# Output projection of a hybrid encoder as a software pipeline over token tiles in fixed order

## The chip, the cores and the metric

The kernel runs on one core of one Trainium2 chip. The metric is the device time of one execution in microseconds (us); the smaller, the better. The program before was run three times: 2376.43, 2377.62 and 2380.9 us, median 2377.62.

## What is computed

Two request groups (prompt and sample, 1024 tokens of 1024 channels each, float32) go through two layers with shared weights: one attention layer (l=0) and one pooling layer (l=1). Cut from the reference:

```python
for l in range(DEPTH):                      # DEPTH = 2
    mod = jax.nn.silu(c) @ ada_w[l] + ada_b[l]
    shift, scl, gate = jnp.split(mod[:, None, :], 3, axis=-1)
    h = _rmsnorm(x, pre_norm[l]) * (1.0 + scl) + shift
    if l % 2 == 0:
        m = _attn_mixer(h, ...)             # ends in y @ w_out
    else:
        m = _pool_mixer(h, ...)             # u, gate = split(h @ w_in); pooled means; gate; y @ w_out
    x = x + gate * _rmsnorm(m, post_norm[l])
```

_rmsnorm divides each token by the root of its mean square and multiplies by a row. Here x after layer 0 is called x1, and the output projection is `y @ w_out` of layer 0 with all that follows it up to h of layer 1.

## The kernel before

Products are made in float32r pairs: each operand is split into a high part and the rest (hi, lo), and one product is three matmuls. `run()` works through four blocks: attention of the prompt group (s=0) and its output projection, attention of the sample group (s=1) and its output projection, then layer 1 of the sample group and layer 1 of the prompt group. `outproj0(s, ...)` (L995) is the output projection. While it works for s=0, it also prepares the attention input of the sample group from x_sample (tiles xo); for s=1 it does not.

It loops over NT = 8 tiles of 128 tokens. For each tile:

- PE forms y @ w_out in PSUM: `out_mm` (L941), for 8 blocks k of channels 6 matmuls of 512 columns, 48 in all (L945 to L947). Tiles 0 and 1 were made ahead, at the end of attention (`out_pre`, L949), whose split y also serves tiles 2 and 3; for tiles 4 to 7 y is loaded and split in `load_y` (L937 to L939).
- ACT squares the result with a sum along each token (L1061), POOL makes the reciprocal root (`rstd`, L123 and L125), DVE multiplies by the gate row (L1063) and adds into the tile xt, which held x (L1064). SP stores xt to DRAM as x1 (L1065).
- `h_tile` (L250 to L265) then norms x1 for layer 1 **in place in xt**: square on ACT (L250), scaling by row g1 on DVE (L252), adding row sh1 on POOL, or on DVE for the last two tiles (L253), eight transposes on PE in two groups (L258), copies to SBUF on ACT (L263) and, where the result is a matmul operand, its lo part on DVE (L265). Since L252 writes what the store L1065 reads, it waits for that store. In s=0 a second `h_tile` does the same for xo with rows g0 and sh0.

For s=1 the results go straight into hT, layer 1's input. For s=0 the halves go to DRAM as a stash (hs_d, 16 stores, L281), and `layer1(0)` reads them back by token tile (L1081), copies hi on ACT (L1083) and forms lo on DVE, some on POOL (L1084). Layer 1 then multiplies hT with its first weights (`lin_both`, L1091 to L1093), copies the first products on ACT (L1122), and works on in four channel groups; the sums of the last output projection of the group before (L1210, L1229 and L1230) fall into the same time.

The engines' order is set by a scheduler, which the language runs over the whole program from the order of the code and its own model of durations. `run_h` (L1019) is a generator that issues the transposes of finished tiles between the matmuls of a later tile. `prefetch` loads and converts weights of the next stage between matmuls (ws, L290 and L291). Each engine runs its instructions in the order that the scheduler left, and SP issues all DMAs, also in that order. A pool with `bufs=n` has n buffers under a tag; a tile that needs a buffer waits until what was in it is used up. xt has two, xo two, yh two, y0 two.

Of the kernel before, what the change touches and what calls it, by code (L numbers as in the profile page):

```python
# [59 lines left out]
class Trunk:  # L60
    def __init__(self, ctx, tc, t):
# [9 lines left out]
        self.pin = False  # L71
# [18 lines left out]
        self.hs_d = self.dram.tile([NT, 2, P, 4, P], F32, name="hs_d")  # L90
# [153 lines left out]

    def h_tile(self, pool, x, g, sh, idm, put, junk=None, eng=None):
        nc = self.nc
        ss = pool.tile([P, 1], F32, name=self.n("ss"), tag="ss", bufs=6)
        if junk is None:
            junk = pool.tile([P, D], F32, name=self.n("jk"), tag="jk", bufs=2)
        nc.scalar.activation(junk, x, AF.Square, accum_out=ss)  # L250
        r = self.rstd(pool, ss, D, 1)
        nc.vector.scalar_tensor_tensor(x, x, r, g, op0=ALU.mult, op1=ALU.mult)  # L252
        (eng or nc.gpsimd).tensor_tensor(x, x, sh, ALU.add)  # L253
        for b in range(2):
            T = self.ptile("T")
            for k in range(4):
                kk = 4 * b + k
                x_ = nc.tensor.transpose(T[:, k * P : (k + 1) * P], x[:, kk * P : (kk + 1) * P], idm)  # L258
                if k == 0 and self.pin:
                    self.tc.keep_in_program_order(x_)  # L260
            hi, lo, done = put(b)
            Tv = T.rearrange("p (k c) -> p k c", k=4)
            nc.scalar.activation(hi, Tv, AF.Copy)  # L263
            if lo is not None:
                nc.vector.tensor_tensor(lo, Tv, hi.bitcast(F32), ALU.subtract)  # L265
            if done:
                done()
            yield

    @staticmethod  # L270
    def put_hT(hT, i):
        def put(b):
            c = slice(i * P, (i + 1) * P)
            return hT[:, 4 * b : 4 * b + 4, 0, c], hT[:, 4 * b : 4 * b + 4, 1, c], None

        return put

    def put_stash(self, pool, i):
        def put(b):
            hl = pool.tile([P, 4, P], F32, name=self.n("hl"), tag="hl", bufs=2)  # L280
            return hl, None, lambda: self.nc.sync.dma_start(self.hs_d[i, b], hl)  # L281

        return put
# [289 lines left out]
    def layer0(self, s, hT, ap, side, after_proj, open2, run_h, first=None):  # L573
# [28 lines left out]
        if s == 1:  # L602
            self.psum("B", "J")
            self.psum("C", "J")
            self.psum("A", "JJ")
            self.raw = [ap.tile([P, 4, 256], F32, name=self.n("raw"), tag="P", bufs=3) for _ in range(2)]
            for f in range(2):
                nc.sync.dma_start(self.raw[f], self.t["win"][9][:, 4 * f : 4 * f + 4, :])
            next(gens[0])
            self.pin = True  # L610
            for _ in gens[0]:
                run_h(1)
            run_h(40)
            self.pin = False
            open2()
# [378 lines left out]

    def outproj0(self, s, wo, op, hN, pre, prefetch):  # L995
# [4 lines left out]
        hq = []  # L1000
        ys, xt, xo = {}, {}, {}

        def load(i):
            if i < NT:
                xt[i] = op.tile([P, D], F32, name=self.n("xt"), tag="xt", bufs=2)
                nc.sync.dma_start(xt[i], xsrc[i])
                if i >= 4:
                    ys[i] = []
                    for f in range(2):
                        y0 = op.tile([P, 4, P], F32, name=self.n("y0"), tag="y0", bufs=2)  # L1010
                        ys[i].append(op.tile([P, 2, 4, P], F32R, name=self.n("yh"), tag="yh", bufs=2))
                        self.load_y(s, i, y0, ys[i][f], 4 * f, 4 * f + 4, 0)

        def load_o(i):
            if s == 0 and i < NT:
                xo[i] = op.tile([P, D], F32, name=self.n("xo"), tag="xo", bufs=2)
                nc.sync.dma_start(xo[i], xos[i // 2, i % 2])

        def run_h(c):  # L1019
            for _ in range(c):  # L1020
                while hq:
                    try:
                        next(hq[0])
                        break
                    except StopIteration:
                        hq.pop(0)

        perm = op.tile([P, P], F32, name=self.n("perm"), tag="perm")
        g1, sh1 = (self.row(op, x) if s == 1 else None for x in ("g1", "sh1"))
        pg = self.mrow(op, 0, s, 2, "pg")  # L1030
        load(0)
        load(1)
        load_o(0)
        if s == 0:
            g0, sh0 = self.mrow(op, 0, 1, 1, "g0"), self.mrow(op, 0, 1, 0, "sh0")
        load(2)
        g1, sh1 = self.mrow(op, 1, s, 1, "g1", g1), self.mrow(op, 1, s, 0, "sh1", sh1)
        nc.sync.dma_start(perm, t["k_perm"])
        pf = prefetch(op)
        for i in range(NT):  # L1040
            if i >= 2:
                load(i + 1)
            load_o(i + 1)
            if i < 2:
                ps = pre[0][i]
                run_h(4)
            else:
                ps = self.ptile("S")
                for k in range(KT):
                    yh, q = (pre[1][i], k) if i < 4 else (ys[i][k // 4], k % 4)  # L1050
                    self.out_mm(ps, yh, q, wo, k, k == 0, k == KT - 1)
                    if k % 2 == 1:
                        run_h(1)
                        if i >= 4:
                            next(pf, None)
            if s == 0:
                jx = op.tile([P, D], F32, name=self.n("jx"), tag="jx", bufs=1)
                hq.append(self.h_tile(op, xo[i], g0, sh0, self.ident, self.put_hT(hN, i), jx))
            ss = op.tile([P, 1], F32, name=self.n("ss"), tag="ss", bufs=6)
            jk = op.tile([P, D], F32, name=self.n("jk"), tag="jk", bufs=1)  # L1060
            nc.scalar.activation(jk, ps, AF.Square, accum_out=ss)  # L1061
            r = self.rstd(op, ss, D, 1)
            nc.vector.tensor_tensor(jk, ps, pg, ALU.mult)  # L1063
            nc.vector.scalar_tensor_tensor(xt[i], jk, r, xt[i], op0=ALU.mult, op1=ALU.add)  # L1064
            nc.sync.dma_start(x1o[i], xt[i])  # L1065
            put = self.put_stash(op, i) if s == 0 else self.put_hT(hN, i)
            hq.append(self.h_tile(op, xt[i], g1, sh1, perm, put, jk, nc.vector if i >= NT - 2 else None))
        for _ in pf:
            pass
        return run_h  # L1070

    def layer1(self, s, hT, lp, hp, run_h, open_l2):
# [4 lines left out]
        if s == 0:  # L1077
            for i in range(NT):
                h = lp.tile([P, 2, 4, P], F32, name=self.n("h"), tag=("sg1", "wa")[i % 2], bufs=2)
                for b in range(2):  # L1080
                    nc.sync.dma_start(h[:, b], self.hs_d[i, b])  # L1081
                    hi, lo = (hT[:, 4 * b : 4 * b + 4, e, i * P : i * P + P] for e in range(2))
# [465 lines left out]
```

## Time and profile before

| | |
|---|---|
| median of three runs | 2377.62 us |
| profiled execution, span on the core | 2374.5 us |
| the part of the median outside that span | 3.1 us |
| PE busy | 2152.6 us, 91% |
| DVE busy | 1569.9 us, 66% |
| ACT busy | 1062.9 us, 45% |
| POOL busy | 1026.7 us, 43% |
| DMA, mean over the span | 77 GB/s |

The profile is of one execution, of which the span is recorded; the 3.1 us are the difference of the median to it. PE is the matmul engine, PEld its weight loads, DVE, ACT and POOL the vector, scalar and general engines, SP the one that issues DMAs (SPq in a row). "[6.87 <-DMA xt<-xp]" behind a row says that the engine stood idle for 6.87 us before it and that the load of xt from xp ended this. PEclk is the clock that was granted to PE, as a share of 2.4 GHz; 0.50 is its other level, 1.2 GHz. The two output-projection stages lie at 800 to 978 us (s=0) and 1650 to 1798 us (s=1); layer 1 of the prompt group begins at about 2060 us.

### The profile page before, as it was taken

To read this page: it belongs to the slowest core of one execution; us is meant where nothing else is said; L and a number is where in the kernel's file an instruction comes from. 1 tells how busy PE (TensorE), PEld (TensorE's weight loads), DVE (VectorE), ACT (ScalarE), POOL (GpSimd) and SP (SyncE) were. 2 spreads that over 40 slices of the span, in tenths; PEclk is the share of its full clock that TensorE was granted. 3 is DMA by queue.
4 is the path that set the end of the run, shared out by engine and by line. 5 is a ranking of instruction groups with operands and counts; after the bars stand their busy time and mean duration, and the time that the engine had idled before them with its cause. 6 is when DMAs were issued, how large, how long until landed. Compare 5 with 4: busy or idle time off the path is not lost.

```text
span 2374.5 us, 38597 instructions
## 1 busy us (share of the span) xinstructions
PE 2152.6 (91%) x13777; PEld 1907.4 (80%) x13777; DVE 1569.9 (66%) x3453; ACT 1062.9 (45%) x2451; POOL 1026.7 (43%) x1455
## 2 busy tenths in 40 slices
PE   5999899999997866899999999988678999999998
PEld 3988788899997655898898999987457888778887
DVE  7788887767778344677878767775344454693536
ACT  6355555766665333355657666664221111310112
POOL 3675663135344253553321234433223345483552
PEclk9999999999997887999999999989789999999999
DMA  6123222112113444210011112124222111441113
GB/s 253 41 65 95 79 86 69 35 54 71 54 47 106 128 134 131 79 37 17 19 34 37 42 57 69 50 82 116 90 73 85 44 45 53 151 164 40 55 44 146
DMA packets 146561, 182.84 MB, mean 77 GB/s; under 512 B 13944, under 2 KB 109280, under 8 KB 146368
## 3 DMA queue, kind: packets, MB, share of 16 engines
q1 hardware_dynamic: 146032, 179.91, 24.1%
q8 instruction: 109, 1.79, 0.3%
q14 instruction: 84, 0.69, 0.1%
q10 hardware_dynamic: 144, 0.26, 0.0%
q0 software_dynamic: 192, 0.20, 0.0%
HBM read 142.33 MB, written 37.99 MB: 76 GB/s over the span
## 4 chain that ended last, share of the span: by engine, by line
PE 53%; DMA 15%; DVE 15%; issue 7%; POOL 6%; ACT 4%; SPq 0%; POOLq 0%; DVEq 0%; ACTq 0%
PE J L355 5%; PE J L357 5%; PE J L356 5%; PE S L1091 4%; PE S L1093 4%; PE S L1092 4%; DMA x_d<-xt 3%; PE H L676 3%; DMA xt<-xp 3%; POOL w L291 3%; PE T L714 2%; DVE E L694 2%; PE S L1186 2%; PE S L1188 2%; PE S L1187 2%
## 5 line engine op out<-in xcount | busy, mean ns | idle before, releaser
L291 POOL TENSOR_TENSOR w<-ws,w 128x256 fp32r<-128x256 f32 (+1 forms) x418 | 391.0, 949 | 360.0 <-DVE w L290 267.1
L355 PE MATMUL J<-w,hT 128*128 128x256 f32 x1664 | 482.5, 290 | 3.2 <-ACT xj L368 2.3
L357 PE MATMUL J<-w,hT 128*128 128x256 f32 x1664 | 477.5, 287 | 4.1 <-DVE hT L1312 3.9
L356 PE MATMUL J<-w,hT 128*128 128x256 f32 x1664 | 477.7, 287 | 0.4 <-POOL w L291 0.4
L355 PEld LDWEIGHTS J<-w,hT 128*128 128x128 f32 x1664 | 318.7, 192 | 7.2 <-ACT xj L368 3.7
L357 PEld LDWEIGHTS J<-w,hT 128*128 128x128 f32 x1664 | 318.5, 192 | 6.8 <-DVE hT L1312 4.6
L356 PEld LDWEIGHTS J<-w,hT 128*128 128x128 f32 x1664 | 318.5, 191 | 2.9 <-POOL w L291 0.9
L693 ACT ACTIVATE E<-T 128x512 fp32r<-128x512 f32 x384 | 226.8, 598 | 207.4 <-PE T L714 67.3
L694 DVE TENSOR_TENSOR E<-T,E 128x512 fp32r<-128x512 f32 x384 | 261.6, 682 | 84.5 <-ACT E L693 82.3
L290 DVE CAST w<-ws 128x256 fp32r<-128x256 f32 (+1 forms) x420 | 196.6, 493 | 169.5 <-PE S L1093 86.0
L683 ACT ACTIVATE P<-H,mx 128x512 f32<-128x512 f32 x256 | 173.7, 685 | 109.9 <-DVE mx L678 95.2
L1093 PE MATMUL S<-hT,w 128*128 128x512 f32 x512 | 200.5, 392 | 2.0 <-POOL w L291 2.0
L1091 PE MATMUL S<-hT,w 128*128 128x512 f32 x512 | 200.7, 392 | 0.0
L1092 PE MATMUL S<-hT,w 128*128 128x512 f32 x512 | 200.3, 391 | 0.0
L677 DVE TENSOR_REDUCE mx<-H 128x1 f32<-128x512 f32 x256 | 173.7, 681 | 34.1 <-PE H L676 32.0
L714 PE MATMUL T<-identr,P 128*128 128x128 f32 x1024 | 162.6, 274 | 6.9 <-DVE mr L151 3.2
L727 PE MATMUL O<-E,v 128*128 128x256 f32 x512 | 142.8, 301 | 14.1 <-DVE E L694 13.5
L793 ACT ACTIVATE P<-H,nm 128x256 f32<-128x256 f32 x256 | 117.7, 474 | 81.2 <-DVE nm L787 81.0
L726 PE MATMUL O<-E,v 128*128 128x256 f32 x512 | 146.1, 294 | 3.9 <-DVE X L748 2.2
L714 PEld LDWEIGHTS T<-identr,P 128*128 128x128 f32 x1024 | 122.4, 141 | 23.9 <-DVE mr L151 3.4
L441 POOL TENSOR_TENSOR hl<-xj,hl 128x256 fp32r<-128x256 f32 x64 | 48.2, 756 | 206.6 <-DVE hl L440 149.5
L727 PEld LDWEIGHTS O<-E,v 128*128 128x128 f32 x512 | 96.8, 189 | 27.2 <-DVE E L694 24.5
(264 smaller groups left out, 5228.8 us busy)
## 6 DMA issues: line engine op xcount, KB each, us to landing
ws<-win SPq DMA_DIRECT2D x192, 128.0 KB
ws<-ada_w SPq DMA_DIRECT2D x128, 128.0 KB
ws<-pwin SPq DMA_DIRECT2D x60, 256.0 KB
vb<-v_d SPq DMA_DIRECT2D x64, 144.0 KB
xt<-xp SPq DMA_DIRECT2D x16, 512.0 KB
ada<-ada_w SPq DMA_DIRECT2D x16, 512.0 KB
y_d<-X SPq DMA_DIRECT2D x32, 256.0 KB
v_d<-v SPq DMA_DIRECT2D x64, 128.0 KB
```

Of the source, the lines that this page charges most:

```text
L290: nc.vector.tensor_copy(hi, src)
L291: (nc.vector if dve_lo else nc.gpsimd).tensor_tensor(lo, src, hi.bitcast(F32), ALU.subtract)
L355: nc.tensor.matmul(ps, hi, w[:, 0, k, :], start=(k == 0), stop=False)
L356: nc.tensor.matmul(ps, hi, w[:, 1, k, :], start=False, stop=False)
L357: nc.tensor.matmul(ps, lo, w[:, 0, k, :], start=False, stop=(k == KT - 1))
L693: nc.scalar.activation(ov[0], Tv, AF.Copy)
L694: nc.vector.tensor_tensor(ov[1], Tv, ov[0].bitcast(F32), ALU.subtract)
L714: nc.tensor.transpose(T[:, (2 * e + i) * P : (2 * e + i + 1) * P], Pt[(h, 2 * g + i)][:, (2 * kp + e) * P : (2 * kp + e + 1) * P], self.ident)
L727: nc.tensor.matmul(O, st["v"][:, kk, :], pairs(ex, 1, e), start=False, stop=(kk == 7))
L1091: nc.tensor.matmul(ps[:, cs], w[:, 0, k, ws], hT[:, k, 0, cs], start=(k == 0), stop=False)
L1092: nc.tensor.matmul(ps[:, cs], w[:, 0, k, ws], hT[:, k, 1, cs], start=False, stop=False)
L1093: nc.tensor.matmul(ps[:, cs], w[:, 1, k, ws], hT[:, k, 0, cs], start=False, stop=(k == KT - 1))
```

## The change

`h_tile`, its two put functions and the pinning flag are gone. `outproj0` writes its whole order out itself, in a region in which the scheduler keeps all engines in program order. Iteration i issues the matmuls of tile i (8 blocks), the post-processing of tile j = i-1, and, between the blocks, the transposes of tile j-1. The norm is written to a tile of its own (hx with two buffers, ho with one), so the store reads xt undisturbed, and xt is reloaded once it is stored. The loads of y are parted from their split (`load_yh`, `split_y`); xo goes from two buffers to one, yh from two to three. Tile 7's transposes go between the first steps of the next stage.

For s=0 hx is normed without row g1 and row sh1. The stash becomes [channel block, 128, tokens]; `layer1(0)` reads it by channel block k, and applies scale and shift there, as columns gc and sc (hc), on ACT for hi and on DVE for the value that lo is taken from. PE's order is fixed as well in `lin_both` and in one unit of the projection behind the stage of s=0. The core of the diff:

```diff
-        self.hs_d = self.dram.tile([NT, 2, P, 4, P], F32, name="hs_d")
+        self.hs_d = self.dram.tile([KT, P, S], F32, name="hs_d")
...
     def outproj0(self, s, wo, op, hN, pre, prefetch):
...
+        def norm(x, junk, g, sh, dve=False):
+            r = square(x, junk)
+            def rest():
+                if g is None:
+                    nc.vector.tensor_scalar_mul(junk, x, r)
+                else:
+                    nc.vector.scalar_tensor_tensor(junk, x, r, g, op0=ALU.mult, op1=ALU.mult)
+                    (nc.vector if dve else nc.gpsimd).tensor_tensor(junk, junk, sh, ALU.add)
+            return rest
...
+        load_x(0)
+        load_o(0)
+        load_x(1)
...
+        region = self.tc.manual_schedule()
+        region.__enter__()
+        for i in range(NT + 1):
+            j = i - 1
+            todo = []
+            if s == 0 and j >= 1:
+                todo += [(trans_o, j - 1, 0), (trans_o, j - 1, 1)]
+            if j >= 1:
+                todo += [(trans_h, j - 1, 0), (trans_h, j - 1, 1)]
...
+            load_yh(i + 1)
+            mm(i, 0)
+            if j >= 0:
+                ps = pss.pop(j)
+                jk = op.tile([P, D], F32, name=self.n("jk"), tag="jk", bufs=1)
+                r = square(ps, jk)
+                nc.vector.tensor_tensor(jk, ps, pg, ALU.mult)
+                tr()
+                nc.vector.scalar_tensor_tensor(xt[j], jk, r, xt[j], op0=ALU.mult, op1=ALU.add)
+                nc.sync.dma_start(x1o[j], xt[j])
+            mm(i, 1)
+            mm(i, 2)
+            tr()
+            if j >= 0:
+                hx[j] = op.tile([P, D], F32, name=self.n("hx"), tag="hx", bufs=2)
+                rest = norm(xt[j], hx[j], g1, sh1, j >= NT - 2)
+            split_y(i + 1, 0)
+            mm(i, 3)
+            mm(i, 4)
+            if i >= 4:
+                next(pf, None)
+            if s == 1 and j >= 0:
+                rest()
+            if s == 0 and j >= 0:
+                ho[j] = op.tile([P, D], F32, name=self.n("ho"), tag="ho", bufs=1)
+                rest_o = norm(xo[j], ho[j], go, so)
+                rest()
+            tr()
+            mm(i, 5)
+            mm(i, 6)
+            if s == 0 and j >= 0:
+                rest_o()
+                load_o(j + 1)
+            tr()
+            split_y(i + 1, 1)
+            mm(i, 7)
+            if i >= 4:
+                next(pf, None)
+            if j >= 0:
+                load_x(j + 2)
...
     def layer1(self, s, hT, lp, hp, run_h, open_l2):
...
+            for k in range(KT):
+                h = lp.tile([P, S], F32, name=self.n("h"), tag=("sg1", "wa")[k % 2], bufs=2)
+                nc.sync.dma_start(h, self.hs_d[k])
+                hi, lo = (hT[:, k, e, :] for e in range(2))
+                gc, sc = hc[1][:, k : k + 1], hc[0][:, k : k + 1]
+                nc.scalar.activation(hi, h, AF.Identity, scale=gc, bias=sc)
+                nc.vector.tensor_scalar(h, h, gc, sc, op0=ALU.mult, op1=ALU.add)
+                (nc.gpsimd if k % 4 == 3 else nc.vector).tensor_tensor(lo, h, hi.bitcast(F32), ALU.subtract)
```

Three places show what moves. On PE, where the stage of s=0 has its first transposes (S is a tile's PSUM, wo the weights, T the transposed half), before:

```order
L945 MATMUL S_10824<-wo_10116,yw_10420 128x512
L946 MATMUL S_10824<-wo_10116,yw_10420 128x512
L947 MATMUL S_10824<-wo_10116,yw_10420 128x512
L945 MATMUL S_10944<-wo_10116,yw_10420 128x512
L946 MATMUL S_10944<-wo_10116,yw_10420 128x512
L947 MATMUL S_10944<-wo_10116,yw_10420 128x512
L258 MATMUL T_10771<-identr,xo_10735 128x128 x4
```

and now:

```order
L904 MATMUL S_10775<-wo_10116,yw_10420 128x512
L905 MATMUL S_10775<-wo_10116,yw_10420 128x512
L906 MATMUL S_10775<-wo_10116,yw_10420 128x512
L904 MATMUL S_10775<-wo_10116,yw_10420 128x512
L905 MATMUL S_10775<-wo_10116,yw_10420 128x512
L906 MATMUL S_10775<-wo_10116,yw_10420 128x512
L959 MATMUL T_10790<-identr,ho_10761 128x128 x4
L904 MATMUL S_10775<-wo_10116,yw_10420 128x512
```

Before, all 48 matmuls of tile 2 and 3 of tile 3 stood ahead of the first transposes of xo, 51 in all; now 6 of tile 2 do (S_10824 before is S_10775 now).

On SP, late in the stage of s=0 (x_d is the store of x1, hs_d the stash, ws weights of the next stage), before:

```order
L1017 DMA xo_11199<-xs 128x1024
L1065 DMA x_d<-xt_11050 4x32x1024
L281 DMA hs_d<-hl_11281 128x512
L306 DMA ws_11284<-win 128x256
L1006 DMA xt_11187<-xp 128x1x1024
L281 DMA hs_d<-hl_11305 128x512
L306 DMA ws_11308<-win 128x256
L1017 DMA xo_11335<-xs 128x1024
L281 DMA hs_d<-hl_11409 128x512
L1065 DMA x_d<-xt_11187 4x32x1024
L1006 DMA xt_11323<-xp 128x1x1024
L281 DMA hs_d<-hl_11429 128x512
```

and now:

```order
L1072 DMA x_d<-xt_11003 4x32x1024
L265 DMA ws_11203<-win 128x256
L1022 DMA hs_d<-hl_11215 128x4x128
L982 DMA xo_11237<-xs 128x1024
L1022 DMA hs_d<-hl_11239 128x4x128
L265 DMA ws_11256<-win 128x256
L977 DMA xt_11260<-xp 128x1x1024
L988 DMA y_1819_11262<-y_d 128x4x128
L988 DMA y_1820_11264<-y_d 128x4x128
L1072 DMA x_d<-xt_11132 4x32x1024
```

Now every iteration has the same ten DMAs, and the reload of xt, with the two loads of y right behind it, comes after the store, the stash and xo.

On DVE, where layer 1 of the prompt group begins (L1084 before, and L1131 and L1132 now, convert the stash; S and m belong to the output of the group before; w<-ws are weights), before:

```order
L1210 TENSOR_TENSOR m_21582<-S_23225,m_21582 128x1024
L1229 SCALAR_TENSOR_TENSOR m_21582<-m_21582,rr_23169,row_21583 128x1024
L1084 TENSOR_TENSOR hT_23327<-h_23357,hT_23327 128x4x128
L1084 TENSOR_TENSOR hT_23328<-h_23357,hT_23328 128x4x128
L1210 TENSOR_TENSOR m_21582<-S_23251,m_21582 128x1024
L1084 TENSOR_TENSOR hT_23327<-h_23378,hT_23327 128x4x128
L1084 TENSOR_TENSOR hT_23327<-h_23371,hT_23327 128x4x128
L1210 TENSOR_TENSOR m_21582<-S_23276,m_21582 128x1024
L1084 TENSOR_TENSOR hT_23328<-h_23371,hT_23328 128x4x128
L1229 SCALAR_TENSOR_TENSOR m_21582<-m_21582,rr_23195,row_21583 128x1024
L1210 TENSOR_TENSOR m_21582<-S_23302,m_21582 128x1024
L290 CAST w_23508<-ws_23509 128x512
```

and now:

```order
L1131 TENSOR_SCALAR h_23369<-h_23369,hc_23346,hc_23345 128x1024
L1132 TENSOR_TENSOR hT_23343<-h_23359,hT_23343 128x1024
L1257 TENSOR_TENSOR m_21598<-S_23318,m_21598 128x1024
L249 CAST w_23515<-ws_23516 128x512
L249 CAST w_23515<-ws_23520 128x512
L249 CAST w_23515<-ws_23524 128x512
L1276 SCALAR_TENSOR_TENSOR m_21598<-m_21598,rr_23262,row_21599 128x1024
L1276 SCALAR_TENSOR_TENSOR m_21598<-m_21598,rr_23287,row_21599 128x1024
L1132 TENSOR_TENSOR hT_23344<-h_23369,hT_23344 128x1024
L1276 SCALAR_TENSOR_TENSOR m_21598<-m_21598,rr_23313,row_21599 128x1024
L1131 TENSOR_SCALAR h_23379<-h_23379,hc_23346,hc_23345 128x1024
L1132 TENSOR_TENSOR hT_23344<-h_23379,hT_23344 128x1024
```

Before, the last conversion stood ahead of the three weight casts; now the last two channel blocks that come over DVE, h_23369 (k=4) and h_23379 (k=6), are finished behind them and behind two and three more L1276 (which were L1229).

## Rows read from the trace of the kernel before

**Rows 1.** Windows: us, busy us (instructions) of PE, PEld, DVE, ACT, POOL; PEclk; DMA share; GB/s.

```profile
800.00:978.00 178.00, 122.66 (x571) 99.23 (x570) 73.68 (x89) 50.55 (x99) 70.03 (x81) 0.83 0.44 135
985.00:1035.00 50.00, 49.59 (x404) 47.75 (x403) 37.44 (x92) 21.15 (x54) 35.63 (x57) 1.00 0.14 44
1650.00:1798.00 148.00, 100.13 (x401) 79.06 (x401) 53.62 (x57) 29.12 (x53) 34.06 (x48) 0.81 0.30 93
1800.00:2040.00 240.00, 240.00 (x1049) 197.03 (x1048) 115.92 (x120) 30.18 (x29) 108.41 (x84) 1.00 0.17 57
```

**Rows 2.** Waits in 800:975 (us in total, times, longest us).

```profile
DVE xt L252 <- DMA x_d<-xt: 51.4, 8, 8.6
```

**Rows 3.** Waits in 1640:1800.

```profile
DVE xt L252 <- DMA x_d<-xt: 57.4, 8, 9.4
```

**Rows 4.** Timeline of DVE (start us, us, engine line op out<-in xcount [idle before <-releaser]).

```profile
813.52 1.28 DVE L1064 SCALAR_TENSOR_TENSOR xt<-jk,rr,xt 128x1024 f32<-128x1024 f32 x1 [6.87 <-DMA xt<-xp]
...
852.29 1.28 DVE L1064 SCALAR_TENSOR_TENSOR xt<-jk,rr,xt 128x1024 f32<-128x1024 f32 x1 [3.52 <-DMA xt<-xp]
...
955.99 0.19 DVE L327 TENSOR_SCALAR g<-g 128x64 f32<-128x64 f32 x1 [4.47 <-DMA g<-gq]
...
956.94 1.27 DVE L1064 SCALAR_TENSOR_TENSOR xt<-jk,rr,xt 128x1024 f32<-128x1024 f32 x1
...
1656.28 1.28 DVE L1064 SCALAR_TENSOR_TENSOR xt<-jk,rr,xt 128x1024 f32<-128x1024 f32 x1 [6.28 <-DMA xt<-xs]
...
1688.20 1.28 DVE L1064 SCALAR_TENSOR_TENSOR xt<-jk,rr,xt 128x1024 f32<-128x1024 f32 x1 [3.12 <-DMA xt<-xs]
...
1746.47 1.28 DVE L1064 SCALAR_TENSOR_TENSOR xt<-jk,rr,xt 128x1024 f32<-128x1024 f32 x1
...
1758.38 1.28 DVE L252 SCALAR_TENSOR_TENSOR xt<-xt,rr,row 128x1024 f32<-128x1024 f32 x1 [7.64 <-DMA x_d<-xt]
...
2061.87 4.62 DVE L1210 TENSOR_TENSOR m<-S,m 128x1024 f32<-128x1024 f32 x4 [2.04 <-PE S L1188]
```

**Rows 5.** Timeline of SP, which issues the DMAs.

```profile
801.37 1.02 SPq L1017 DMA_DIRECT2D xo<-xs  x1
...
943.16 1.01 SPq L326 DMA_DIRECT2D g<-gq  x1
...
1679.34 0.59 SPq L1006 DMA_DIRECT2D xt<-xs  x1
...
1747.78 0.54 SPq L1065 DMA_DIRECT2D x_d<-xt  x1
```

**Rows 6.** Timeline of POOL.

```profile
1759.81 2.68 POOL L253 TENSOR_TENSOR xt<-xt,row 128x1024 f32<-128x1024 f32 x1 [9.96 <-DVE xt L252]
```

**Rows 7.** Transposes L258 in 820:980: duration ns min/median/max, first and last start us.

```profile
L258 PE MATMUL T<-perm,xt x64: 270/273/476, 840.4 to 977.1; 128*128 128x128 f32 x64
```

**Rows 8.** Timeline of ACT.

```profile
821.59 1.06 ACT L250 ACTIVATE jx<-xo 128x1024 f32<-128x1024 f32 x1 [16.57 <-DMA xo<-xs]
...
2097.57 1.03 ACT L1122 ACTIVATE u<-S 128x1024 f32<-128x1024 f32 x1 [4.41 <-PE S L1093]
```

**Rows 9.** Timeline of PE.

```profile
1796.19 1.97 PE L258 MATMUL T<-perm,xt 128*128 128x128 f32 x8 [8.03 <-DVE xt L253]
```

**Rows 10.** Groups of DVE by form in 2035:2130 (busy us, mean ns; idle before, releasers).

```profile
L1229 DVE SCALAR_TENSOR_TENSOR m<-m,rr,row 128x1024 f32<-128x1024 f32 x8 | 15.4, 1948 | 0.4 <-POOL rr L125 0.4
...
L1210 DVE TENSOR_TENSOR m<-S,m 128x1024 f32<-128x1024 f32 x8 | 9.5, 1214 | 2.0 <-PE S L1188 2.0
```

**Rows 11.** Windows behind the first products of layer 1, s=0 (columns as in rows 1).

```profile
2098.00:2112.00 14.00, 11.99 (x46) 9.44 (x46) 11.78 (x7) 0.60 (x1) 14.00 (x8) 0.88 0.74 251
2112.00:2130.00 18.00, 16.35 (x71) 12.96 (x70) 17.92 (x13) 3.95 (x4) 14.25 (x13) 1.00 0.34 119
```

**Rows 12.** Windows within the stage of s=0 (columns as in rows 1).

```profile
840.00:845.00 5.00, 2.89 (x20) 2.35 (x19) 2.48 (x3) 2.61 (x5) 1.45 (x2) 1.00 0.27 79
860.00:865.00 5.00, 0.00 (x0) 0.00 (x0) 0.83 (x1) 0.00 (x0) 0.00 (x0) 0.72 0.54 176
```

More of the change, by code (lines that the diff above doesn't have):

```diff
@@ L70, in __init__ @@
         self.uid = 0
-        self.pin = False
         self.raw = None
@@ L243, in mrow @@
         return r
[L245 to L283, printed above, removed]
     def split(self, hi, lo, src, dve_lo=False, act=False):
@@ L608, in layer0 @@
                 nc.sync.dma_start(self.raw[f], self.t["win"][9][:, 4 * f : 4 * f + 4, :])
[L609 to L614, printed above, removed]
+            with self.tc.manual_schedule(engines={mybir.EngineType.PE}):
+                next(gens[0])
+                for i, _ in enumerate(gens[0]):
+                    if i in (2, 3, 6, 7):
+                        run_h(1)
+                run_h(40)
             open2()
@@ L993, in out_pre, with trans_half @@
         return mms, finish
+    def trans_half(self, x, b, idm, hi, lo, done=None):
+        nc = self.nc
+        T = self.ptile("T")
+        for k in range(4):
+            kk = 4 * b + k
+            nc.tensor.transpose(T[:, k * P : (k + 1) * P], x[:, kk * P : (kk + 1) * P], idm)
+        Tv = T.rearrange("p (k c) -> p k c", k=4)
+        nc.scalar.activation(hi, Tv, AF.Copy)
+        if lo is not None:
+            nc.vector.tensor_tensor(lo, Tv, hi.bitcast(F32), ALU.subtract)
+        if done:
+            done()
     def outproj0(self, s, wo, op, hN, pre, prefetch):
@@ L999, in outproj0, with load_x @@
         x1o = self.x1_d[s].rearrange("(t m r) d -> t r m d", m=32, r=4)
-        hq = []
-        ys, xt, xo = {}, {}, {}
-        def load(i):
+        xt, xo, hx, ho, y0, yh, pss = {}, {}, {}, {}, {}, {}, {}
+        def load_x(i):
             if i < NT:
@@ new lines, in square @@
+        def square(src, junk):
+            ss = op.tile([P, 1], F32, name=self.n("ss"), tag="ss", bufs=6)
+            nc.scalar.activation(junk, src, AF.Square, accum_out=ss)
+            return self.rstd(op, ss, D, 1)
+        def norm(x, junk, g, sh, dve=False):
[7 more added lines that the diff above has]
+            return rest
@@ L1019, in run_h @@
+        for _ in pf:
+            pass
+        region.__exit__(None, None, None)
+        rest_t = [(f, NT - 1, b) for f in ((trans_o, trans_h) if s == 0 else (trans_h,)) for b in range(2)]
         def run_h(c):
             for _ in range(c):
[L1021 to L1067, printed above, removed]
@@ L1068, in outproj0 @@
-        for _ in pf:
-            pass
+                if rest_t:
+                    f, n, b = rest_t.pop(0)
+                    f(n, b)
         return run_h
@@ L1102, in lin_both @@
             pss = [self.ptile("S") for _ in range(2)]
-            for c in range(2):
-                for ct in range(2):
-                    lin_c(pss[ct], w, ct, c)
-                    if c == 0 and run_h:
-                        run_h(2)
-                if c == 0 and open_l2:
-                    open_l2()
+            with self.tc.manual_schedule(engines={mybir.EngineType.PE}):
+                for c in range(2):
+                    for ct in range(2):
+                        lin_c(pss[ct], w, ct, c)
+                    if c == 0 and open_l2:
+                        open_l2()
             return pss
```

61 lines of the change are left out of this document (47 added, 14 removed).

## The prediction

> **What bounds the kernel now.** I read the windows by stage first. In the stretches that follow the two output-projection stages PE is busy all the time (49.59 of 50 us, 240.00 of 240 us [rows 1]). In the stages themselves it is not: 122.66 us of 178 for the prompt group (s=0), 100.13 us of 148 for the sample group (s=1), at a mean granted clock of 0.83 and 0.81. These two holes, some 103 us of idle PE, are all the change can reach.
>
> The waits say what the holes are. The costliest in both stages is DVE's norm (L252), held by the store of the same tile (x_d<-xt): eight times, 51.4 and 57.4 us [rows 2, 3]. The timelines show one such round for s=1. DVE writes x1 into xt at 1746.47 [rows 4], SP issues its store at 1747.78 [rows 5], and only at 1758.38, 10.6 us after the issue, may L252 overwrite xt [rows 4]; then POOL adds the shift (1759.81, 2.68 us [rows 6]) and the transposes may run. The buffer comes back only after them, so the next load is late too. One tile follows the next by 20.9 us in s=0 (852.29 to 956.94, five tiles) and by 19.4 us in s=1 (1688.20 to 1746.47, three) [rows 4].
>
> PE's own work is shorter. A 512-column matmul costs 240.00/1049 = 0.229 us [rows 1], and 48 of them 11.0 us; one transpose 0.273 us [rows 7], a group of four 1.09 us. A tile of s=0 has 16 transposes, 4.4 us, of s=1 half as many, 2.2 us: **15.4 and 13.2 us** are the floors.
>
> **The change, part by part.**
>
> *Norm out of place.* It takes the store out of the path to the transposes: L252's 10.6 us wait goes. What is late next is the reload. Two xt buffers remain, so load_x(j+2) waits for the store of tile j, and SP takes its DMAs in order: the y tiles for iteration i+2 stand right behind that load. Over two iterations: x1 is written about 5 us into the first, the store lands some 10.6 us later, SP issues the loads (0.8 us), they land after L, then come the split of y and six small steps (square 1.06 us [rows 8], reciprocal about 1, scaling 1.28 [rows 4], POOL's add 2.68 [rows 6]), 6.6 us in all. So 2T = 21.8 + L for s=0 and, with no xo norm in between, 20.4 + L for s=1, less what of these steps falls behind PE's next matmuls. For L I take 8.7 us, an xt load from issue at 1679.34 to its use at 1688.20 [rows 4, 5]; the other end is 20.2 us, the first xo load (issue 801.37, use 821.59 [rows 5, 8]), with nine transfers under way. L=8.7 gives T=15.3 for s=0, just PE's floor, and 14.5 for s=1. In s=0 more is queued: the stash stores, xo, weights, and a weight cast in front of DVE's next product (0.6 to 3 us). There I take L about 11 and T=17 in the three full iterations, 16 before them and 15.8 after.
>
> *Fixed order, s=0.* PE now meets the first transposes six matmuls into tile 2, where it had 51 matmuls in front of them. They wait for the norm of the first xo. That load now stands ahead of the second xt; the first xt was used at 813.52 [rows 4], so xo lands about then, and the steps above put the transposes at about 820 (815 to 828): some 12 us of PE are lost at once. The rest of tile 2 (42 matmuls, 16 transposes: 14 us) ends at 834, tiles 3 to 7 (16+17x3+15.8=82.8) at 917; 1.7 us, an estimate, for the low clock after the first wait: 918.5. Tile 7's norms then sit behind the scaled rope rows on DVE, which wait for g<-gq; that load needs the weights' space, so it is issued only when PE is done with tile 7. Before, it took 12.8 us from issue (943.16) to use (955.99) [rows 4, 5]; here, with less traffic, I take 7 (3.5 to 12.8), and ho of tile 7 is ready at about 937. PE has 8.8 us of transposes and 127 projection matmuls of 0.123 us (49.59/404 [rows 1]; so many stand ahead of the last transposes before), 15.6 us, and an 8 us hole: 951, against 978, where the last transposes ended (their last start: 977.1 [rows 7]). **Gain 27 us (20 to 36).**
>
> *Fixed order, s=1.* The first xt is used at 1656.28 [rows 4], its transposes at about 1662, in place of PE's run of matmuls from 1650; tile 2 ends at 1674, four iterations of 14.5 and one of 13.2 reach 1745, low clock 1.7. Then come 48 matmuls of the next layer, 11.0 us, four groups of transposes, 4.4, and 1.5 for the scale column, which waits for its own load: 1763.5, against 1798.2, where the last transposes ended [rows 9]. **Gain 35 us (29 to 40).**
>
> *Stash without scale and shift.* Layer 1 of the prompt group now applies them when it reads the stash: eight more passes on DVE (L1131). ACT's copies only change form, and ACT is idle half of this time. Before, a token tile was converted by itself, so the first token half could start with four of them; now a block of the stash is one channel block of all tokens, and PE's first product needs all eight. In DVE's order the seventh, k=6, comes 29 instructions after 2061.87 [rows 4]: 26 passes over 1024 elements (8 of L1210's kind, 7 of L1229's, 11 new) and 3 casts. At L1210's 1.21 us for each [rows 10] that is 35 us, to 2097. From k=6 PE has 78 matmuls, 17.8 us: the first pair of products ends at 2115, where ACT's copy of it began at 2097.57 before [rows 8]. PE idled 2.0 and 1.7 us just behind this [rows 11], and DVE's pile of passes is worked off by then, so some 4 us come back: **loss 13 us (5 to 20)**. The low end is with DVE passes at 0.75 of that, the high end with seven at L1229's mean of 1.95 us [rows 10]. L1229 ran at 1.95 while POOL was adding all the time, L1210, which reads one operand from PSUM, at 1.21. The Trainium skill says why (GPSIMD Engine Reference, Key points): POOL shares its SBUF interfaces with VectorE and collides with instructions that have two SBUF inputs. The trace agrees [rows 10]; were all 26 passes stretched so, the loss would be about 32 us and the sum 2350.
>
> *Small things.* The stash's stores go from 2 KB runs to 512 B, awaited only a tile later by their two buffers; their cost is hidden by T=17. Two loads of single elements (hc) stand on SP ahead of weights: 2 us (0 to 5). Fewer rows are loaded for s=0: nothing, since those landed while attention's last matmuls ran.
>
> **Sum:** -27 - 35 + 13 + 2 = -47 us. The profiled execution spans 2374.5 us, 3.1 under the median of 2377.62; that part lies around the span and does not change. 2377.6 - 47 = **2330 us**.
>
> **Rivals.**
>
> *A. Layer 1 hides the affine* (chance 0.17). PE has other products until DVE is through; L1229's passes could fall in PE's shadow, and 26 at 1.21 is the price only if the order holds. Then the 13 us stay: 2317.
>
> *B. The clock stays low* (0.14). PE still pauses in each iteration, about 1.7 us in s=0. For it: the stages ran at 0.83 and 0.81 [rows 1]. Against it: in 840 to 845 PE idled 2.1 us in short pieces and the granted clock stayed at 1.00, one level of the two, while the emptier 860 to 865 brought 0.72 [rows 12]. If it stays near 0.82, T grows by about 2.5 us in 10 iterations: 2355. The Trainium skill holds waits for DMA between groups of matmuls to be what brings the clock back to half (TensorE: Matmul & The Clock Gate, Loop structure matters more than you think); the trace [rows 12] agrees for the long holes only.
>
> *C. Slower: the transfers take over* (0.06). Everything late in the pipe hangs on one chain, store then load then norm, and it is closed over two buffers. If L is not 9 to 11 us but what the first xo took, 20.2, T becomes 21 in s=0 and 20.3 in s=1, as long as the old tile: five iterations in each cost 22 and 30 us more than forecast, and the sum is +5. The point is L=19; each microsecond above it costs half of one in ten iterations. At L=21 the time is 2387. For it: a DMA share of 0.44 over the stage of s=0, three times that of the stretch behind it [rows 1]. Against it: after that start the loads land in 9 to 15 us.
>
> *D. The change does nothing* (0.03): PE's order is written, but another wait of equal length (the y split, yh's three buffers) takes the store's place at about T=20: about 2377.
>
> **How the numbers follow.** The forecast has 0.60: 2330. Its own ends are 2330-9-5-8-2=2306 (all gains at the upper end, the loss at its lower) and 2330+7+6+7+3=2353. Rival A lies inside; B at 2355 sets the upper end. Range **2304 to 2358**, which leaves out some 0.15, the worst of B, C and D. A measurement of this kernel can tell about 0.2%, 5 us, from no change. Faster by more: forecast, A and B, 0.91, and a little of C and D: 0.92. Within: half of D and some of C, 0.02. Slower: 0.06.
>
> **What would show it.** Right: no wait on x_d<-xt in DVE's table except at the reload on SP; tiles 17 us apart in s=0 and 14.5 in s=1; a hole on PE of some 12 us at the first transposes of each stage, and one before tile 7's; PE clock near 1.00 between; last transposes at about 951 and, shifted by s=0's gain, 1737; in layer 1 of the prompt group, PE waiting for DVE's pass of k=6. Wrong: tiles still 20 us apart, with loads of xt or y as what ends the waits (C); holes short but clock at 0.8 (B); the first pair's ACT copy no later than before, counted from the end of the other group (A).

## The result and the profile after

The changed kernel takes **2418.0 us** (median of four runs, 2417.26 to 2418.41) against 2378.89 us for the kernel before (2376.43 to 2380.9): a ratio of **1.0169, 95% interval 1.0154 to 1.0183**. It is 39 us slower; forecast were 47 us less, 2330 us, in a range that ended at 2358.

The windows of the two stages, columns as in [rows 1]:

```profile
800.00:985.00 185.00, 120.86 (x564) 99.24 (x563) 59.74 (x85) 52.84 (x104) 52.76 (x71) 0.81 0.43 124
1670.00:1820.00 150.00, 105.97 (x441) 83.31 (x441) 58.65 (x63) 33.08 (x62) 37.88 (x51) 0.85 0.32 94
```

PE is as idle as before: 64 us in s=0 and 44 us in s=1 (55 and 48 in the shorter windows of [rows 1]); its granted clock is at 0.81 and 0.85. The waits of s=0 and then those of s=1 (us in total, times, longest us); in the first row of each pair PE waits for POOL's part of the norm ahead of its transposes:

```profile
PEld T L959 <- POOL ho L1010: 59.5, 7, 15.2
...
DVE w L249 <- DMA ws<-win: 43.6, 8, 9.4
```

```profile
PEld T L959 <- POOL hx L1010: 35.9, 5, 14.6
...
DVE w L249 <- DMA ws<-pwin: 27.7, 8, 6.7
```

In the kernel before, the same casts (L290 there) waited far less, s=0 (800 to 1000):

```profile
DVE w L290 <- DMA ws<-win: 5.0, 5, 3.1
```

DVE's waits for the store of x1 [rows 2, 3] are gone, as forecast. In their place DVE waits for weights of the next stage (ws), which it has only to cast: eight times in s=0, and in s=1 once in each of the last four tiles (the other four of that row's eight lie behind the stage). One tile of s=0, first DVE and then SP (columns as in [rows 4, 5]):

```profile
889.14 1.29 DVE L1071 SCALAR_TENSOR_TENSOR xt<-jk,rr,xt 128x1024 f32<-128x1024 f32 x1
...
899.97 0.29 DVE L249 CAST w<-ws 128x256 fp32r<-128x256 f32 x1 [4.64 <-DMA ws<-win]
900.18 0.75 DVE L1007 TENSOR_SCALAR hx<-xt,rr 128x1024 f32<-128x1024 f32 x1
902.45 1.28 DVE L1009 SCALAR_TENSOR_TENSOR ho<-xo,rr,row 128x1024 f32<-128x1024 f32 x1 [1.52 <-POOL rr L124]
...
909.60 0.29 DVE L249 CAST w<-ws 128x256 fp32r<-128x256 f32 x1 [5.27 <-DMA ws<-win]
909.81 1.22 DVE L1069 TENSOR_TENSOR jk<-S,row 128x1024 f32<-128x1024 f32 x1
...
911.66 1.28 DVE L1071 SCALAR_TENSOR_TENSOR xt<-jk,rr,xt 128x1024 f32<-128x1024 f32 x1
```

```profile
890.46 0.55 SPq L1072 DMA_DIRECT2D x_d<-xt  x1
891.12 0.40 SPq L265 DMA_DIRECT2D ws<-win  x1
...
903.76 0.34 SPq L982 DMA_DIRECT2D xo<-xs  x1
...
904.68 0.44 SPq L265 DMA_DIRECT2D ws<-win  x1
```

This is a closed ring. x1 of a tile is written at 889.14; its store and then a load of weights go out on SP (890.46, 891.12); the load is used at 899.97, 8.9 us after its issue, and the cast that waits for it stands ahead of both norms (900.18, 902.45). Only when the second norm has read xo may SP reload xo (903.76), and only behind that comes the second load of weights (904.68), used at 909.60; and behind *its* cast stand the product and x1 of the next tile (911.66). Two loads in a row and what lies between make 22.5 us a tile, where 17 were forecast. (From one store of x1 to the next SP has nine DMAs here, not the ten that I counted when I described the change.) In s=1 there is one such wait in each tile, and the tile takes 18.3 us (1754.82 to 1773.10), where 14.5 were forecast:

```profile
1754.82 1.27 DVE L1071 SCALAR_TENSOR_TENSOR xt<-jk,rr,xt 128x1024 f32<-128x1024 f32 x1
...
1765.85 0.29 DVE L249 CAST w<-ws 128x256 fp32r<-128x256 f32 x1 [4.59 <-DMA ws<-pwin]
...
1773.10 1.28 DVE L1071 SCALAR_TENSOR_TENSOR xt<-jk,rr,xt 128x1024 f32<-128x1024 f32 x1
```

Behind the stage of s=0 comes a loss that the prediction did not have. The weights of the third projection unit are loaded as one group of 16. Before, it went out at 989.52, 11 us behind the last transposes; now at 1012.69, 28 us behind them, and PE idles 11.9 of the 30 us from 1015 on, against 0.3 before. SP before, SP now, PE in the first 15 of these before, PE now:

```profile
989.52 33.84 SPq L306 DMA_DIRECT2D ws<-win  x16
```

```profile
1012.69 21.73 SPq L265 DMA_DIRECT2D ws<-win  x16
```

```profile
1015.00:1030.00 15.00, 14.72 (x120) 13.82 (x119) 11.36 (x28) 7.66 (x19) 11.00 (x19) 1.00 0.22 69
```

```profile
1015.00:1030.00 15.00, 8.34 (x65) 7.53 (x64) 11.42 (x27) 3.06 (x9) 13.77 (x22) 0.88 0.30 90
1030.00:1045.00 15.00, 9.81 (x62) 9.42 (x62) 10.01 (x25) 3.98 (x10) 7.84 (x13) 0.67 0.13 37
```

In layer 1 of the prompt group PE waits for the converted stash, as forecast, and ACT's copies of the first two products follow late; PE, ACT, DVE, and then POOL and SP:

```profile
2106.40 0.79 PE L1140 MATMUL S<-hT,w 128*128 128x512 f32 x1 [6.81 <-DVE hT L1132]
...
2115.53 0.79 PE L1140 MATMUL S<-hT,w 128*128 128x512 f32 x1 [6.20 <-DVE hT L1132]
```

```profile
2138.99 1.03 ACT L1169 ACTIVATE u<-S 128x1024 f32<-128x1024 f32 x1 [17.05 <-PE S L1141]
...
2144.57 1.00 ACT L1169 ACTIVATE u<-S 128x1024 f32<-128x1024 f32 x1
```

```profile
2084.01 3.48 DVE L1257 TENSOR_TENSOR m<-S,m 128x1024 f32<-128x1024 f32 x3 [4.90 <-PE S L1235]
...
2112.12 3.35 DVE L1132 TENSOR_TENSOR hT<-h,hT 128x1024 fp32r<-128x1024 f32 x1
...
2121.97 1.46 DVE L1131 TENSOR_SCALAR h<-h,hc,hc 128x1024 f32<-128x1024 f32 x1 [2.67 <-ACT hT L1130]
2123.47 1.22 DVE L1132 TENSOR_TENSOR hT<-h,hT 128x1024 fp32r<-128x1024 f32 x1
```

```profile
2111.13 3.26 POOL L1277 TENSOR_TENSOR xt<-xt,m 128x1024 f32<-128x1024 f32 x1
```

```profile
2114.42 0.33 SPq L1278 DMA_DIRECT2D ys<-xt  x1
2114.80 0.42 SPq L1266 DMA_DIRECT2D xt<-x_d  x1
2115.32 0.74 SPq L1127 DMA_DIRECT2D h<-hs_d  x1
```

The channel block k=6 is through at 2124.7, 40.7 us after DVE began its pile at 2084.01; forecast were 35. For 2.7 of these DVE waits for ACT's copy of that block, whose load from the stash SP issues only at 2115.32, behind a store (ys) that waits for POOL's add. The second copy comes 60.6 us after 2084.01; before, 35.7 us lay between 2061.87 [rows 4] and 2097.57 [rows 8].

To see where the time went in each run, I cut every trace at four marks: the last store of y of each group (y_d, SP), and the second copy of u on ACT in layer 1 of each group.

| us | before | changed | change | forecast |
|---|---|---|---|---|
| A: stage of s=0 and attention of s=1 (y_d to y_d) | 843.7 | 868.1 | +24.4 | -27 |
| B: stage of s=1, to u | 168.0 | 157.7 | -10.3 | -35 |
| C: layer 1 of the sample group, to u of the prompt group | 287.0 | 316.3 | +29.3 | with D: +13 |
| D: from there to the end | 276.9 | 270.7 | -6.2 | |

C and D together are 23.1 us longer. The remaining 3.6 us lie ahead of A, in attention that both kernels run in the same order; the runs below scatter there by as much (799.5 to 803.5 us, 798.9 before), and I have no cause for it.

### The profile page after: what moved, and what is told of

Its sections match the earlier page's. It is cut to its first block, busy times and chain, and to the rows that moved or that the text cites. A ratio compares the mean times of both kernels' runs of the same rounds, so it can differ in the third digit from the quotient of the medians.

```text
span 2415.3 us, 38531 instructions
## 1 busy us (share of the span) xinstructions
PE 2155.3 (89%) x13777; PEld 1910.0 (79%) x13777; DVE 1553.9 (64%) x3453; ACT 1064.9 (44%) x2443; POOL 1014.0 (42%) x1447
## 3 DMA queue, kind: packets, MB, share of 16 engines
q1 hardware_dynamic: 152816, 178.87, 24.1%
## 4 chain that ended last, share of the span: by engine, by line
PE 54%; DVE 16%; DMA 12%; POOL 6%; issue 6%; ACT 4%; SPq 1%; POOLq 0%; DVEq 0%; ACTq 0%
PE J L314 5%; PE J L315 5%; PE J L316 5%; PE S L1140 5%; PE S L1141 5%; PE S L1139 5%; DMA ws<-win 4%; PE H L635 3%; POOL w L250 2%; PE T L673 2%; DVE E L653 2%; PE S L1233 2%; PE S L1234 2%; PE S L1235 2%; DVE mx L636 2%
## 5 line engine op out<-in xcount | busy, mean ns | idle before, releaser
L636 DVE TENSOR_REDUCE mx<-H 128x1 f32<-128x512 f32 x256 | 173.9, 682 | 43.6 <-PE H L635 41.7
L1140 PEld LDWEIGHTS S<-hT,w 128*128 128x128 f32 x512 | 97.1, 190 | 37.5 <-DVE hT L1132 16.6
```

The costliest lines, as they stand in the source:

```text
L636: nc.vector.tensor_reduce(mx[:, c : c + 1], ps[c], axis=AX, op=ALU.max, negate=True)
L1140: nc.tensor.matmul(ps[:, cs], w[:, 0, k, ws], hT[:, k, 1, cs], start=False, stop=False)
```

## The experiments

The kernel before was measured again beside them: 2377.36 us beside e1 to e4, 2381.53 beside e5 to e8 and 2381.21 beside e9 to e12. The sums below are differences of medians; across these groups they are certain to some 4 us only.

Theory, from the trace: the weight loads close a ring over DVE and SP; the fixed order of the projection unit holds up the weights behind it; the affine on the stash costs what was forecast or more. Rival for the first: the ring is the prediction's own, store, reload of xt and load of y, and the casts only wait beside it.

**e1_ws_ahead.** Weight loads two ahead of their casts, on two buffers for s=0 where there was one, the first two at the end of iteration 3:

```diff
+        load(0); load(1); yield
+        for q in range(KT):
+            self.split(w[:, 0, q : q + 1], w[:, 1, q : q + 1], ws[q])
+            load(q + 2)
+            yield
```

> The changed kernel, with the weight loads of the prefetch (ws) issued two ahead of their casts on two buffers for s=0 (three for s=1), so that a cast on DVE finds its data there. Theory (a ring: x1 in DVE, store and ws load on SP, cast on DVE, norms, xo load and second ws load, second cast, next x1): the tile period in iterations 4 to 7 falls from 22.7 to about 17 us in s=0 and from 18.4 to about 14.5 us in s=1, together some 35 us less than the changed kernel: 2383 us (2375 to 2395). Rival (the ring is store, reload of xt and load of y, and the cast waits only beside it): the period stays over 20 and 17 us, another wait takes the cast's place, at most 8 us less: 2410 or more.

Measured: 2393.67 us (2389.39 to 2397.01), 24 less than the changed kernel; A falls to 853.3, B to 148.0. DVE's waits for ws in s=0 fall from 43.6 us to next to nothing:

```profile
DVE w L249 <- DMA ws<-win: 1.5, 3, 0.7
```

But a tile of s=0 still takes 19.7 us (882.26 to 941.25, three tiles) and of s=1 16.9 (1716.08 to 1766.65, three tiles). The theory holds for the cause, but brought 24 of its 35 us, and the periods end just under the rival's 20 and 17: something else takes over at 19.7 us, which e6 finds.

**e2_rows_first.** Two rows of s=1 allocated ahead of the gate row:

```diff
+        g1, sh1 = (self.row(op, x) if s == 1 else None for x in ("g1", "sh1"))
         pg = self.mrow(op, 0, s, 2, "pg")
```

> The changed kernel with the two rows of the sample stage (g1, sh1) allocated ahead of the gate row, as the kernel before had it; nothing else moves. Theory (the gate row took a place that PE still reads, so its load, the loads of xt behind it on SP and the first product wait): the load is issued right behind the last store of attention, some 6 us earlier, and the stage ends 6 to 10 us earlier: 2408 to 2412 us. Rival (the first norm waits for the row g1 and xt anyway): within 3 us of the changed kernel.

Measured: 2415.54 us, ratio 1.0155 (1.0137 to 1.0172), which overlaps that of the changed kernel: not told apart by time. In the trace B is 153.0, 4.7 us less, and the first transposes start 24.0 us after the last y store, not 28.6. So by this one trace the late row is a cost, of half the size I expected at best; the rival holds in part too, since the first norm still waits 5.3 us for its own row.

**e3_evac.** Scale and shift applied as ACT copies the transposed halves out of PSUM; stash and layer 1 as before, the two loads of hc in the stage:

```diff
+            for k in range(4):
+                kk = 4 * b + k
+                nc.scalar.activation(hi[:, k], Tv[:, k], AF.Identity, scale=cols[1][:, kk : kk + 1],
+                                     bias=cols[0][:, kk : kk + 1])
```

> The changed kernel with layer 1's scale and shift of the prompt group applied in the stage, by ACT as it copies the transposed halves from PSUM (four copies of 128 columns each in place of one of 512), and the stash and its reading in layer 1 as in the kernel before. Theory (the affine by channel block on DVE delays layer 1 of the prompt group): the 19 to 25 us that this group starts later by go, the stage itself stays as slow: 2396 us (2390 to 2403). Rival (DVE's pile of passes at that place comes from the output of the group before and not from the affine): at most 6 us less, 2412 or more. If ACT's eight small copies for one lengthen the ring of the stage, that costs up to 1.5 us a tile, 12 us.

Measured: 2402.31 us, 16 less. C is 287.05, to a tenth what it was before; D is 279.6, and A and B are 2 us longer each. The affine, with the stash by channel block, cost some 20 us in layer 1, and 16 on balance.

**e4_all.** The three together.

> All three edits together. Theory: they lie in different places and add: 35 + 8 + 20 us less than the changed kernel, 2355 us (2340 to 2370), under the kernel before. Rival (what one wait gives, the next takes): above 2378.

Measured: 2366.85 us, ratio to before 0.995 (0.9934 to 0.9966): faster than before, and 51 us under the changed kernel, more than the 24 + 2 + 16 of the single edits. A was still 853.4, 10 us over the kernel before. ACT's split now waited for y (24.1 us in s=0), and DVE for the split. ACT's split of y and SP's load of it (the row of SP is the issue of the load that ends the second wait):

```profile
897.87 0.63 ACT L1020 ACTIVATE yh<-y 128x512 fp32r<-128x512 f32 x1 [2.88 <-DMA y<-y_d]
...
917.56 0.63 ACT L1020 ACTIVATE yh<-y 128x512 fp32r<-128x512 f32 x1 [4.62 <-DMA y<-y_d]
```

```profile
907.78 1.02 SPq L1014 DMA_DIRECT2D y<-y_d  x2
```

The load goes out at 907.78, last in its tile behind xo, the second weights and xt, and is used at 917.56, 9.8 us later; the split, the cast and the norms stand behind it, and behind those the next xo. 19.7 us lie between the two splits: this is the ring that e1 left.

**e5_kv.** e4_all, the scheduler orders the first projection unit behind the stage again:

```diff
-            with self.tc.manual_schedule(engines={mybir.EngineType.PE}):
-                next(gens[0])
-                for i, _ in enumerate(gens[0]):
-                    if i in (2, 3, 6, 7):
-                        run_h(1)
-                run_h(40)
+            next(gens[0])
+            self.pin = True
+            for _ in gens[0]:
+                run_h(1)
+            run_h(40)
+            self.pin = False
```

> The kernel with all three edits (e4_all, 2367 us), and the fixed PE order of the first projection unit behind the stage of s=0 undone: the scheduler orders it again, as before, with tile 7's transposes pinned. Theory (the unit now runs to its end before the next may start, so the weights of the unit after next are loaded 10 us later, at 999 and not at 989 us, and PE loses 11.6 us between 1000 and 1025 us, where it lost 0.3 before): 8 to 12 us less, 2357 us. Rival (tile 7's late norms are the loss and PE only waits elsewhere): within 3 us of 2367.

Measured: 2340.97 us, 26 less; A falls from 853.4 to 827.8. The group of 16 loads goes out at 978.24. The theory holds in its cause; the order costs twice what the one idle window showed.

**e6_y_early.** e4_all, each half of y loaded as soon as its buffer is split:

```diff
-            load_yh(i + 1)
...
             split_y(i + 1, 0)
+            load_yh(i + 2, (0,))
```

> e4_all with each half of y loaded as soon as its buffer is split, half an iteration earlier, and not behind the reload of xt. Theory (with the casts served, the ring is: y load, split on ACT and DVE, the norms behind it in their order, xo load, second weight load, reload of xt, next y load): the period falls from 19.3 to 16 or 17 us in s=0 and from 16 to about 14.5 in s=1, 15 to 25 us less: 2347 us. Rival (store and reload of xt are the ring, which the prediction's 2T = 21.8 + L says): at most 6 us less, 2361 or more.

Measured: 2342.57 us, 24 less; A 840.0, B 132.0. From the third x1 of s=0 to the eighth 79.7 us pass (846.27 to 925.97), 96.2 in e4. They are uneven: one interval of 23.4 us, in which the first weight cast waits 7.9 us for its load, and behind it 15.5, 13.1 and 12.3. Store and reload of xt are not the ring.

**e7_first.** e4_all, all of tile 2's matmuls ahead of the first transposes:

```diff
+            if i == 2:
+                for k in range(1, KT):
+                    mm(i, k)
```

> e4_all with all 48 matmuls of tile 2 ahead of the first transposes in each stage. Theory (PE stands idle for 15 us in each stage while the first norm is made, and 42 matmuls, 9.6 us, fit there): 8 us less in each stage, 2351 us. Rival (the tiles behind are spaced by their own ring, so an earlier tile 2 only waits later): at most 5 us less.

Measured: 2368.71 us (2364.21 to 2373.24), no gain. PE shows why, first of e4_all, then here:

```profile
828.18 1.12 PE L979 MATMUL T<-identr,ho 128*128 128x128 f32 x4 [14.48 <-POOL ho L1036]
...
842.66 0.66 PE L979 MATMUL T<-identr,ho 128*128 128x128 f32 x4 [0.18 <-POOL ho L1036]
```

```profile
827.50 1.97 PE L979 MATMUL T<-identr,ho 128*128 128x128 f32 x8 [4.65 <-POOL ho L1036]
...
841.98 1.11 PE L979 MATMUL T<-identr,ho 128*128 128x128 f32 x4 [9.73 <-POOL ho L1036]
```

The wait of 14.5 us ahead of the first transposes shrinks to 4.7, and the next transposes, which hardly waited (0.2 us), now wait 9.7: the rival holds, tile by tile the norms set the time.

**e8_all.** e4_all with all three.

> e4_all with the three edits of e5_kv, e6_y_early and e7_first. Theory: 10 + 20 + 16 us less than 2367, with some overlap: 2325 to 2345 us. Rival (DVE's own work in the tile, or the reload of xt, becomes the ring): above 2350.

Measured: **2314.54 us, ratio to before 0.9722 (0.9706 to 0.9737)**, 10 us below the range I had given, since e5's edit alone brings 26 and not 10; e5's and e6's gains add up, and e7's is nothing. It is the lowest median of all, though e12's interval below overlaps it. A is 814.6 and B 132.5.

**e9_kv_only and e10_y_only.** The edits of e5 and e6 alone, on the changed kernel.

> The changed kernel with only the fixed PE order of the first projection unit behind the stage of s=0 undone (the scheduler orders it, tile 7's transposes pinned). Theory (this order costs what it cost under the three edits, 26 us, whatever the stage ahead does): 2392 us (2386 to 2399), the stretch from the last y store of s=0 to that of s=1 falls from 868 to about 843 us. Rival (it only cost that much because the stage ahead had become faster): at most 12 us less, 2406 or more.

> The changed kernel with only the loads of y issued as soon as their buffer is split. Theory (the weight casts close the ring, and y is not part of it): the tile period stays near 22.7 us in s=0 and 18.4 us in s=1, within 5 us of 2418. Rival (the waits for y and for the weights stand in series): 15 to 24 us less, as under the three edits, 2394 to 2403.

e9: 2395.31 us, 23 less, A 841.6: the group of 16 loads goes out at 985.15, not 1012.69:

```profile
985.15 35.65 SPq L266 DMA_DIRECT2D ws<-win  x16
```

So this order cost as much in the changed kernel itself. e10: 2426.41 us, 8 *more* by the medians and 6 when each is set against the kernel before beside it; the two ratios, 1.0194 (1.0179 to 1.0209) and 1.0169 (1.0154 to 1.0183), just touch. The trace shows where: A is 8.4 us longer. The waits for ws rise from 43.6 to 62.3 us, and a tile takes 25.0 us (888.88 to 913.91): y is outside the ring, as the theory says, but its load now stands on SP ahead of the weight load that the ring waits for, which the theory had missed:

```profile
DVE w L249 <- DMA ws<-win: 62.3, 8, 13.6
```

```profile
890.20 0.55 SPq L1071 DMA_DIRECT2D x_d<-xt  x1
892.63 0.37 SPq L988 DMA_DIRECT2D y<-y_d  x1
893.11 1.93 SPq L265 DMA_DIRECT2D ws<-win  x1
```

**e11_best and e12_best_nofirst.** e8_all with the first weight loads one iteration earlier; e12 also without e7's edit.

```diff
-            if i == 3:
+            if i == 2:
                 next(pf)
```

> All edits (e8_all, 2314.5 us), with the first two weight loads issued one iteration earlier still. Theory (the first cast of the stage of s=0 waited 7.8 us for a load that was issued 9 us before it, all behind it waited too): 5 to 8 us less in each stage, 2302 us (2298 to 2308). Rival (another load takes its place): within 4 us of 2314.

> e11_best with the transposes of the first tile back between the matmuls of tile 2, as the change has them. Theory (42 matmuls fit into PE's wait, and with the rings gone the earlier tile 2 is now worth something): 5 to 15 us more than e11_best. Rival (as in e7_first, tile 3 waits for its own norm in both): within 4 us of it.

Measured: 2319.94 (2315.45 to 2324.43) and 2316.13 us (2312.59 to 2317.48): no gain over e8, whose interval both overlap, and e7's edit is worth nothing here either. In e11 the tiles of s=0 from tile 2 on are even, 15.3 to 16.0 us, next to the 15.4 that I had worked out as PE's floor, up to tile 7, which then waits for the scaled rope rows. DVE and SP:

```profile
918.56 1.23 DVE L1107 TENSOR_TENSOR jk<-S,row 128x1024 f32<-128x1024 f32 x1 [1.71 <-ACT jk L1028]
928.69 0.20 DVE L307 TENSOR_SCALAR g<-g 128x64 f32<-128x64 f32 x1 [8.91 <-DMA g<-gq]
...
932.25 1.27 DVE L1109 SCALAR_TENSOR_TENSOR xt<-jk,rr,xt 128x1024 f32<-128x1024 f32 x1
```

```profile
919.45 0.82 SPq L306 DMA_DIRECT2D g<-gq  x1
```

Tile 7's x1 is written at 932.25, as in e8 (932.69): what the earlier tiles won is lost to g<-gq, issued at 919.45 and used 9.2 us later. That is the end of the stage that the prediction described. In s=1 e11's last tile takes 19.3 us (15.6 in e8), for which I have no cause.

## Why the prediction was wrong, point by point

- *The store's wait goes*: right. DVE never waits for x_d in the changed kernel.
- *The tile period* (17 and 14.5 us): wrong, and the step that failed most. I took "a weight cast in front of DVE's next product (0.6 to 3 us)". There were two casts a tile in s=0, the first ahead of the norms, and each waited 4.6 to 9.4 us for a load that the fixed order put directly ahead of it. I had built the ring from store, reload and y, and not followed the ws loads through SP, where each stands behind an instruction that waits for DVE. With the casts fed (e1) 24 us came back. Next in size, once the casts are fed, was y itself (e6, 24 us; alone, in e10, the same edit gained nothing): I put its load in the formula with L = 8.7 to 11 us after the reload of xt, and the formula gave 17, but in e4 the two splits lay 19.7 us apart, since SP issued the reload behind xo, the stash and the second weights: 17.9 us behind x1 (889.24 to 907.17), and not as soon as the store had landed. The formula's own terms (5, 10.6, 0.8 and 6.6) add up to 23.0 and not 21.8; that is 0.6 us a tile and not what failed.
- *The fixed order of the projection unit*: left out; it was worth 23 us (e9) and 26 (e5). I had counted PE's work up to the last transposes and ended the sum there; what came late was the next but one unit, whose weights wait for the buffer that this unit reads.
- *The affine in layer 1*, 13 us (5 to 20): right in mechanism, and too small in size: C and D took 23.1 us more, of which e3 gave back 20, and 16 by time, since its stages took 4 longer. The pile took 40.7 us and not 35. Some 3 of the difference are waits, 2.7 of them for the late stash load of k=6, an order on SP again. The rest I put down to passes stretched beside POOL: the one of L1132 at 2112.12 took 3.35 us and ended 1.1 us after POOL's add (2111.13, 3.26 us), the last took 1.22. This agrees with what the Trainium skill states of the shared SBUF interfaces (GPSIMD Engine Reference, Key points), where instructions with two SBUF inputs are the ones concerned. It did not reach all 26 passes, as the 32 us of the prediction supposed: the eight of L1257, with one input in PSUM, still took 1.21 us.
- *The start of the stages*: the first transposes came 25.5 and 28.6 us after the last y store (828.0 and 1699.2), not 21 and 19.5. PE's holes there were 14.5 and 13.9 us, where 12 were expected. In s=0 it was the row g0 that landed last, at 824.27, and not xo; in s=1 the late gate row accounts for 4.6 of the 9.1 us (e2), and the row of the first norm, for which DVE waits 5.3 us more, is still there.
- *The wait for g<-gq at tile 7*, 8 us: hidden in the changed kernel, where tiles are late anyway (0.2 us), and there once they are not (8.9 us of waiting in e11).
- *Small things*, 2 us: no run takes out the two loads of hc by themselves, so this term is neither confirmed nor refuted.
- *Rival C* had the right sign and the right shape, a ring of transfers as long as the old tile, with a chance of 0.06; but it named the reload of xt, and the ring was closed by the weights. *Rival B*: the clock was low (0.81, 0.85), by my reading as a consequence: with PE waiting up to 15 us ahead of a tile's transposes, long holes like that of [rows 12] remained. It fits that in e8, with shorter waits, the stages are at 0.91 (800 to 985) and 0.92 (1614 to 1747), and the whole span at 0.970 against 0.949; no run changes the clock alone.

Where the things that I had costed at little or nothing are taken away, the stages end about where the forecast had them: in e8 A is 29.1 us under the kernel before (forecast 27) and B 35.5 (forecast 35), without the affine's 13. That they meet so closely is in part luck: e8 does not load y behind the reload of xt, as the formula has it, and its tiles of s=0 do not follow by 16 to 17 us but mostly by 13 to 16, with two intervals of 23 (the first weight load and g<-gq).

## What to carry to other kernels

A hand-written order fixes every engine's queue, so a small instruction in it that waits for a transfer holds all that stands behind it: for each load, follow who issues it, behind what, and who waits for its use, and issue it at least one landing time ahead. A scheduler did most of that here unasked (its weight casts of s=0 waited 5.0 us in all, those of the written order 43.6); where it is switched off, the side work (prefetch, constants, the unit that follows) must be placed with the same care as the main loop. And a sum that ends at a milestone leaves out what the same edit does to the stage behind it.

## What was not expected of the hardware

A load of 128 KB took very different times from its issue to the cast that waited for it, by its place in SP's order: 8.9 us behind the 512 KB store of x1 (891.12 to 899.97), 4.9 us behind a stash store and xo (904.68 to 909.60). The eight loads of the stage of s=0 in the changed kernel divide so throughout: 8.9 to 12.0 us directly behind a store of x1, 4.3 to 4.9 in the other place. Whether it is the store, or the load of xt (with y, but for the last) that went out 5 to 8 us earlier, that makes the difference, no run separates.
